# Late modulation groups on column quarters of TensorE, an earlier zero fill, and a merged exponent product in a diffusion-block kernel

## The chip, the core and the metric

The kernel runs on one core of a Trainium2 chip. A core has five engines, each with its own instruction queue that is worked off in order: TensorE (PE, matrix products; its weight loads are listed as PEld), VectorE (DVE), ScalarE (ACT), GpSimd (POOL) and SyncE (SP, which here issues nearly all DMAs; 16 DMA engines carry them out). Between engines only semaphores order the work. The metric is the time of one execution on the device in microseconds (us); the median of three runs of the kernel before is 1539.05 us.

## The reference, cut to what matters

One trunk layer over 256 context tokens and 1024 latent tokens of width 1024: adaptive modulation of a norm, one input projection (3096 columns) that feeds three head groups (RWKV-7, Mamba-2 SSD, gated linear attention, GLA), an output projection, and a mixture of experts.

```python
cond_l = jax.nn.silu(c); cond_c = jax.nn.silu(c_ctx)[None]
mod_l = jnp.split(cond_l @ ada_w[l] + ada_b[l], 6, -1)     # 1024 x 6144 weights
mod_c = jnp.split(cond_c @ ada_w[l] + ada_b[l], 6, -1)
hl = modulate(rmsnorm(x, norm1_g[l]), mod_l[0], mod_l[1])
hc = modulate(rmsnorm(ctx, norm1_g[l]), mod_c[0], mod_c[1])
mc, ml = mixer(hc, hl, ...)          # h @ w_in, then rwkv7 | ssd | gla, both directions
x = x + mod_l[2][:, None] * ml
x = x + mod_l[5][:, None] * hier_moe(modulate(rmsnorm(x, norm2_g[l]), mod_l[3], mod_l[4]), ...)
return rmsnorm(x, final_g)
```

The modulations are 6144 columns, worked in 12 groups of 512. Groups 0 to 3 (shift and scale of the first norm) are needed before anything else. Groups 4 to 11 (`mod_l[2]` to `mod_l[5]`) are needed only from the output projection on. In the SSD part, `decay_in = exp(a_cs[l] - a_cs[s])` over chunks of 128 tokens is the exponent product of the change.

## The kernel before

**Stages, by the profiled execution.** To 52 us inputs are loaded and transposed, the first four modulation groups computed (`ada_first`, L150, with plain matmuls at L163) and the first norm applied. From 52 to 564 us the projection stage runs (below). From 564 to 738 us the RWKV chain runs: 20 calls of `rw_step`, each a sequence of 64x64 matmuls on data that `rw_loads` (L575 on) fetches from DRAM (`cd`, `sm`, `v`), with GLA states and SSD states beside it. From 738 to 905 us `rw_finish`, `ssd_weights` and `gla_out` follow; then the output projection to about 1037 us, routing, and the experts from 1068 us to the end.

**The projection stage** is a list of jobs, the string PLAN. Job s is a block of RWKV heads (projections, then five calls of `rw_seg`, whose elementwise part is on DVE), z, q and c are projections (c with a 3x3 convolution on DVE, L739), g the gate, i the inversion of small triangular blocks (`rw_inverse`, 32x32 matmuls `px`), t the token-major projection (`pst`), and a is one late modulation group. Every fp32 projection is three matmuls on split operands (`mm3`, L261 to L263, result `psi` or `pst`); its weights come through `load_split`: a DMA into `wraw`, a tile of the pool wst with three buffers, then a split into `whi` and `wlo`. A framework schedules the instructions when the kernel is built: it simulates a timeline and writes each engine's order. On the chip each engine follows that order and waits where its next instruction is not ready.

**A late modulation group before** (`ada`, L178): four DMAs of 512 KB bring `wada`, which takes the same three buffers as `wraw`. DVE multiplies and adds the eight row blocks into `aacc` (one L188, seven L190), PE sums over partitions with four matmuls against a column of ones (`psa`, L193; each is two instructions), and L194 adds the bias. The eight groups stand between s0 and c0 in PLAN.

**Zeros and constants.** `rw_zeros` (L353) fills part of the DRAM tensor `sD` with zeros out of a tile of the pool tmp, which can only be opened once the pool st is closed. `ssd_consts2` (L947) then builds the constant part of `difD` (8 planes of 128x128 for each of 8 chunks) in `dift` and writes it. Both precede the first job.

**The exponent.** `ssd_dt` (L981) computes cumulated decays, splits each into three bf16 parts, and writes them into `difD` with 48 DMAs (L1056 to L1058). `ssd_weights` (L1115) loads `df` and makes the exponent of each direction as a mask product (L1135) plus two products over 36 rows (L1137, L1139), followed by the exponential on ACT (L1141).

## Time and profile before

| | us |
|---|---|
| median of 3 runs | 1539.05 (1538.52 to 1543.27) |
| the profiled execution | 1533.99 |
| its span (first to last instruction) | 1532.2 |
| PE busy in the span | 1340.5 (87%) |
| DVE busy | 785.2 (51%) |
| ACT busy | 515.4 (34%) |
| POOL busy | 389.5 (25%) |

The shares are averages over stages that have different limits, so they say little about one change. Of PE two things must be read beside its busy time: the clock that was granted in a stretch (1.00 is 2.4 GHz, 0.50 is 1.2 GHz), since at the lower level the same work shows twice the busy time; and whether the engine's next instruction was waiting, and for whom. Durations of single matmuls overlap with the next, so the step from one start to the next is the cost in a row of them.

### The profile page before, as it was taken

The numbers are of one execution on the slowest core, as the hardware profiler recorded it, in microseconds if no ns is written. First come the engines' busy times: TensorE is split into PE (matmuls) and PEld (weight loads), VectorE is DVE, ScalarE is ACT, GpSimd is POOL, SyncE is SP. The second block draws the span as 40 slices with busy tenths as digits, with TensorE's granted clock in tenths as the row PEclk, the third lists the DMA queues.
The fourth block names the chain that finished last, engine by engine and source line by source line (L and its number), as shares of the span: only waits on it lengthen the run. The fifth ranks groups of instructions, "written<-read, shape, count | busy, mean of one in ns | idle before, by whom it ended". The sixth has DMA issues, their size and how long they took to land. (4 is left out here: it accounts for less than half of the span.)

```text
span 1532.2 us, 28018 instructions
## 1 busy us (share of the span) xinstructions
PE 1340.5 (87%) x11077; PEld 1111.9 (73%) x11077; DVE 785.2 (51%) x1482; ACT 515.4 (34%) x1056; POOL 389.5 (25%) x432
## 2 busy tenths in 40 slices
PE   7897899999797776777889989993999999999984
PEld 3585677777676774666557767762999999999984
DVE  4849868889979854414564472227102212112532
ACT  5544334443363134422433352220212212212333
POOL 3312432343334111413453252112101111111112
PEclk9997899999899777889856589995999999999998
DMA  9454867677661467476544365425988868868984
GB/s 320 134 156 138 201 153 169 167 189 180 162 144 31 93 141 203 127 229 207 185 145 118 97 208 171 145 97 193 368 299 288 271 201 301 294 224 299 311 266 123
DMA packets 297253, 296.81 MB, mean 194 GB/s; under 512 B 114281, under 2 KB 214890, under 8 KB 297119
## 3 DMA queue, kind: packets, MB, share of 16 engines
q1 hardware_dynamic: 288095, 269.81, 57.7%
q0 software_dynamic: 7872, 20.97, 5.7%
q10 hardware_dynamic: 1152, 4.19, 0.7%
q8 instruction: 89, 1.46, 0.4%
q14 instruction: 45, 0.37, 0.1%
HBM read 221.44 MB, written 73.72 MB: 193 GB/s over the span
## 5 line engine op out<-in xcount | busy, mean ns | idle before, releaser
L1576 PE MATMUL p<-hT,w 128*128 128x144 f32 (+10 forms) x2048 | 263.2, 288 | 0.0
L1576 PEld LDWEIGHTS p<-hT,w 128*128 128x128 f32 x2048 | 257.6, 192 | 0.6
L262 PE MATMUL psi<-hlo,whi 128*128 128x512 f32 (+1 forms) x440 | 172.0, 391 | 5.0 <-DVE hlo L234 3.8
L261 PE MATMUL psi<-hhi,whi 128*128 128x512 f32 (+1 forms) x440 | 170.3, 389 | 0.0
L263 PE MATMUL psi<-hhi,wlo 128*128 128x512 f32 (+1 forms) x440 | 169.9, 387 | 0.3 <-POOL wlo L254 0.3
L1583 PE MATMUL p<-hid,w 128*128 128x144 f32 (+10 forms) x1024 | 136.6, 294 | 8.4 <-DVE hid L1578 7.2
L1583 PEld LDWEIGHTS p<-hid,w 128*128 128x128 f32 x1024 | 133.9, 199 | 9.0 <-DVE hid L1578 7.5
L1602 POOL DMA_INDIRECT acc<-yr,rows x27 | 41.4, 1532 | 323.0 <-DVE yr L1598 188.2
L1578 DVE TENSOR_TENSOR hid<-hid,p 128x144 f32<-128x144 f32 (+10 forms) x64 | 18.7, 294 | 170.0 <-PE p L1576 165.9
L262 PEld LDWEIGHTS psi<-hlo,whi 128*128 128x128 f32 x440 | 85.6, 195 | 26.0 <-DVE hlo L234 5.6
L263 PEld LDWEIGHTS psi<-hhi,wlo 128*128 128x128 f32 x440 | 85.4, 194 | 19.1 <-issue 3.4
L261 PEld LDWEIGHTS psi<-hhi,whi 128*128 128x128 f32 x440 | 85.8, 195 | 17.7 <-issue 2.1
L1598 DVE TENSOR_SCALAR yr<-pty,rows 128x512 f32<-128x512 f32 (+8 forms) x46 | 32.7, 741 | 112.4 <-PE pty L1592 105.2
L1584 ACT ACTIVATE yT<-p,mods 128x144 f32<-128x144 f32 (+10 forms) x128 | 43.0, 374 | 112.7 <-PE p L1583 112.5
L1577 ACT ACTIVATE hid<-p 128x144 f32<-128x144 f32 (+10 forms) x64 | 18.2, 284 | 168.8 <-PE p L1576 168.7
L739 DVE SCALAR_TENSOR_TENSOR co<-gr,pc,co 128x512 f32<-128x512 f32 x72 | 59.4, 849 | 6.5 <-ACT co L728 4.7
L190 DVE SCALAR_TENSOR_TENSOR aacc<-wada,csig,aacc 128x512 f32<-128x512 f32 x56 | 51.6, 921 | 15.6 <-DMA wada<-in_ada_w_dram 15.3
L262 PE MATMUL pso<-wol,mh 128*128 128x512 f32 x128 | 52.8, 412 | 3.3 <-DVE wol L1222 2.2
L261 PE MATMUL pso<-woh,mh 128*128 128x512 f32 x128 | 52.4, 412 | 1.0 <-DVE go L1265 1.0
L263 PE MATMUL pso<-woh,ml 128*128 128x512 f32 x128 | 52.6, 411 | 0.0
L463 PE MATMUL psg<-AR,BK 64*128 64x128 f32 x320 | 46.6, 304 | 4.0 <-DVE BK L456 1.6
L463 PEld LDWEIGHTS psg<-AR,BK 64*128 64x128 f32 x320 | 39.5, 204 | 13.4 <-issue 4.0
(540 smaller groups left out, 2668.3 us busy)
## 6 DMA issues: line engine op xcount, KB each, us to landing
w<-in_moe_w_dram SPq DMA_DIRECT2D x47, 2048.0 KB
wada<-in_ada_w_dram SPq DMA_DIRECT2D x32, 512.0 KB
cd<-stepD SPq DMA_DIRECT2D x20, 768.0 KB
wraw<-in_w_in_dram SPq DMA_DIRECT2D x24, 512.0 KB
aw<-in_ada_w_dram SPq DMA_DIRECT2D x10, 512.0 KB
stepD<-AR SPq DMA_DIRECT2D x40, 128.0 KB
mabD<-G SPq DMA_DIRECT2D x40, 128.0 KB
stepD<-G SPq DMA_DIRECT2D x40, 128.0 KB
```

Source lines behind the costliest of these rows:

```text
L190: nc.vector.scalar_tensor_tensor(acc, w[:, k % 2], g.sg[:, k, 0:1], acc, op0=OP.mult, op1=OP.add)
L261: nc.tensor.matmul(ps, whi(k), xhi(k), start=k == 0, stop=False)
L262: nc.tensor.matmul(ps, whi(k), xlo(k), start=False, stop=False)
L263: nc.tensor.matmul(ps, wlo(k), xhi(k), start=False, stop=k == 7)
L463: nc.tensor.matmul(pg[h][:, c, :], bkf[HS[h], c], arf[HS[h], c], start=True, stop=True)
L739: nc.vector.scalar_tensor_tensor(o, src(dy, dx), w(3 * dy + dx), o, op0=OP.mult, op1=OP.add)
L1576: nc.tensor.matmul(p[:, 0:n], w[:, k, fs], hT[:, k, s0:s0 + n], start=k == 0, stop=k == 7)
L1578: nc.vector.tensor_mul(hid[:, f, 0:n], hid[:, f, 0:n], p3[:, 0:n])
L1583: nc.tensor.matmul(p[:, 0:n], w2[:, f, 128 * k:128 * k + 128], hid[:, f, 0:n], start=f == 0, stop=f == 3)
L1584: nc.scalar.activation(yT[:, k, 0:n], p[:, 0:n], AF.Copy, scale=g.mods[:, 40 + k, 0:1])
L1598: nc.vector.tensor_scalar(yr[0:m, h], pf, wt[0:m, b:b + 1], None, op0=OP.mult)
L1602: nc.gpsimd.indirect_dma_start(out=g.acc, out_offset=bass.IndirectOffsetOnAxis(ap=rows[0:m, 0, b:b + 1], axis=0), in_=yr[0:m, :], in_offse ...
```

## The change

- **Late modulations on quarters.** `ada` no longer uses DVE. `sgz` holds the eight blocks of the condition vector, each widened to 32 columns of which only the first is not zero. A matmul with such a block as weights (128x32) and `wada` as the moving operand (128x512) uses a quarter of the array's columns, and block k goes to quarter k%4, partitions 32*(k%4) on, of one PSUM tile; so eight matmuls, two on each quarter, replace the eight DVE operations. ACT copies the tile to `arow`, four matmuls with `sel` (ones at partitions 0, 32, 64, 96) sum the quarters and turn the row into a column (`psc`), DVE adds the bias.
- **Where they stand.** In PLAN the groups 4 to 11 go from between s0 and c0 to between c0 and t0. `wada` moves from the pool wst to buffers of tmp that `rw_seg` no longer needs then (tags G, two, and kk, one).
- **Zeros.** The zero tile `z32` is a persistent one that DVE clears in `gla_consts`, so the `sD` fills don't wait for tmp; SP now issues them among the loads of `x` and `ada_w`. `ssd_consts2` comes after job s0.
- **Exponent.** Rows 36 to 47 of each 64-row half of `difD` carry what had planes 6 and 7. L1137 and L1139 become one product over 48 rows, and `difD` has 6 planes. `ssd_dt` writes its parts once to a DRAM tensor `partsD` and from there with 24 DMAs, DRAM to DRAM, into `difD`.

```diff
+    g.sgz = P.tile([128, 8, 32], F, name="sgz")
+    nc.gpsimd.memset(g.sgz, 0.0)
+    nc.vector.tensor_copy(g.sgz[:, :, 0:1], sg[:, :, 0:1])
+    g.sel = P.tile([128, 1], F, name="sel")
+    nc.vector.tensor_reduce(g.sel, g.ident[:, ::32], axis=AX.X, op=OP.add)
...
-def ada(g, grs):
-    for gr in grs:
-        acc = g.wst.tile([128, 512], F, tag="aacc", name="aacc", bufs=1)
-        for k in range(8):
-            if k % 2 == 0:
-                w = g.wst.tile([128, 2, 512], F, tag="wraw", name="wada", bufs=3)
-                nc.sync.dma_start(w, dap(g.a["ada_w"], 128 * 6144 * k + 512 * gr, [[6144, 128], [128 * 6144, 2], [1, 512]]))
-            if k == 0:
-                nc.vector.tensor_scalar(acc, w[:, 0], g.sg[:, 0, 0:1], None, op0=OP.mult)
...
-                nc.vector.scalar_tensor_tensor(acc, w[:, k % 2], g.sg[:, k, 0:1], acc, op0=OP.mult, op1=OP.add)
-        ps = g.ps.tile([128, 512], F, tag="mm", name="psa")
-        for j in range(4):
-            nc.tensor.matmul(ps[:, j:j + 1], acc[:, 128 * j:128 * j + 128], g.onesm[:, 0:1], start=True, stop=True)
+def ada(g, gr):
+    nc, W = g.nc, g.tmp
+    ps = g.ps.tile([128, 512], F, tag="tp", name="psa")
+    for k in range(8):
+        if k % 2 == 0:
+            g.nada = getattr(g, "nada", 0) + 1
+            if g.nada % 3:
+                w = W.tile([128, 1024], F, tag="G", name="wada", bufs=2)
             else:
+                w = W.tile([128, TT], F, tag="kk", name="wada", bufs=1)[:, 0:1024]
+            w = w.rearrange("p (k f) -> p k f", k=2)
+            nc.sync.dma_start(w, dap(g.a["ada_w"], 128 * 6144 * k + 512 * gr, [[6144, 128], [128 * 6144, 2], [1, 512]]))
+        o = slice(32 * (k % 4), 32 * (k % 4) + 32)
+        nc.tensor.matmul(ps[o, :], g.sgz[:, k, :], w[:, k % 2, :], start=k < 4, stop=k >= 4)
+    row = W.tile([128, 512], F, tag="sa", name="arow", bufs=2)
+    nc.scalar.activation(row, ps, AF.Copy)
+    pt = g.ps.tile([128, 4], F, tag="tp", name="psc")
+    for j in range(4):
+        nc.tensor.matmul(pt[:, j:j + 1], row[:, 128 * j:128 * j + 128], g.sel, start=True, stop=True)
+    nc.vector.tensor_add(g.mods[:, 4 * gr:4 * gr + 4, 0], pt, g.c("adab", 4 * gr, 4))
...
 def rw_zeros(g):
-    z = g.tmp.tile([32, 32], F, name="z32")
-    nc.gpsimd.memset(z, 0.0)
+    z = g.z32
...
-    g.difD = g.dram.tile([8, 128, 8, 128], BF, name="difD")
-    t = g.tmp.tile([128, 8, 128], BF, tag="rv", name="dift", bufs=1)
+    g.difD = g.dram.tile([8, 128, 6, 128], BF, name="difD")
+    t = g.tmp.tile([128, 6, 128], BF, tag="t1", name="dift", bufs=1)
...
+    pD = g.dram.tile([3, 128, 3, 128], BF, name="partsD")
+    nc.sync.dma_start(pD.rearrange("k p i t -> p k (i t)"), parts.rearrange("p k i t -> p k (i t)"))
     for d in range(2):
         for q in range(2):
             for h in range(4):
-                src = parts[64 * d + 4 * q + h:64 * d + 64:8]
-                o = 64 * q + 3 * h
-                nc.sync.dma_start(g.difD[:, o + 12 * d:o + 12 * d + 3, h], src[:, 0])
-                nc.sync.dma_start(g.difD[:, o + 24:o + 27, 4 + d], src[:, 2])
-                nc.sync.dma_start(g.difD[:, o + 24:o + 27, 6 + d], src[:, 1])
+                o = 64 * q + 12 * d + 3 * h
+                nc.sync.dma_start(g.difD[:, o:o + 3, h], pD[0, 64 * d + 4 * q + h:64 * d + 64:8])
+            for r, k in ((24, 2), (36, 1)):
+                nc.sync.dma_start(g.difD[:, 64 * q + r:64 * q + r + 12, 4 + d],
+                                  pD[k, 64 * d:64 * d + 64].rearrange("(c q h) i t -> q c (h i) t", q=2, h=4)[q])
...
-    K = [slice(64 * q, 64 * q + 36) for q in range(2)]
+    K = [slice(64 * q, 64 * q + 48) for q in range(2)]
...
         for q in range(2):
-            nc.tensor.matmul(pe[q].rearrange("p h t -> p (h t)"), df[K[q], 4 + d], R[q], start=False, stop=False)
-        for q in range(2):
-            nc.tensor.matmul(pe[q].rearrange("p h t -> p (h t)"), df[K[q], 6 + d], R[q], start=False, stop=True)
+            nc.tensor.matmul(pe[q].rearrange("p h t -> p (h t)"), df[K[q], 4 + d], R[q], start=False, stop=True)
...
-PLAN = "s0 a9 z0 a4 a5 z1 a7 s1 z3 q0 z2 a6 z5 z4 a11 q1 c1 a8 i0 g0 i2 a10 c0 c3 c2 c5 t0 i1 c4"
+PLAN = "s0 z0 z1 s1 z3 q0 z2 z5 z4 q1 c1 i0 g0 i2 c0 a4 a5 c3 a6 a7 c2 a8 a9 c5 a10 a11 t0 i1 c4"
...
-    ssd_consts2(g)
...
+    for i, job in enumerate(PLAN.split()):
+        if i == 1:
+            ssd_consts2(g)
```

What this does to the engines' orders is shown at three places. The line numbers of the changed kernel are 12 to 17 higher than those of the kernel before: L201 is the matmul on a quarter, L206 the sum with `sel`, L274 to L276 are `mm3`, L475 and L490 are L463 and L478 of before.

PE in the first RWKV block (`psl`, `ptv`, `psg`, `ptb` are steps of `rw_seg`), before:

```order
L426 MATMUL psl<-wa,wa_495 128x256
L193 MATMUL psa<-onesm,aacc 128x1 x4
L463 MATMUL psg<-AR,BK 128x128 x8
L426 MATMUL psl<-wa,wa_495 128x256 x2
L478 MATMUL ptb<-ident,BK 128x128 x4
L419 MATMUL ptv<-ident,rv 128x128 x2
L463 MATMUL psg<-AR,BK 128x128 x4
L426 MATMUL psl<-wa,wa_495 128x256
L463 MATMUL psg<-AR,BK 128x128 x4
L419 MATMUL ptv<-ident,sq 128x128 x2
L193 MATMUL psa<-onesm,aacc 128x1 x4
L261 MATMUL psi<-hhi,whi 128x512
```

The same place after:

```order
L275 MATMUL psi<-hlo,whi 128x512
L490 MATMUL ptb<-ident,BK 128x128 x4
L475 MATMUL psg<-AR,BK 128x128 x4
L438 MATMUL psl<-wa,wa_500 128x256
L431 MATMUL ptv<-ident,rv 128x128 x2
L276 MATMUL psi<-hhi,wlo 128x512
L274 MATMUL psi<-hhi,whi 128x512
```

Before, the steps of `rw_seg` stood bare, with two `psa` groups that need DVE's `aacc` between them; after, `psi` products of z0 and z1 stand between the steps (14 to 21 rows at a time), and no `psa`.

PE where the convolution projections end and the token-major projection begins, before:

```order
L261 MATMUL psi<-hhi,whi 128x512
L262 MATMUL psi<-hlo,whi 128x512
L263 MATMUL psi<-hhi,wlo 128x512
L261 MATMUL pst<-thi,hhi 128x280
L262 MATMUL pst<-tlo,hhi 128x280
```

and after:

```order
L274 MATMUL psi<-hhi,whi 128x512
L275 MATMUL psi<-hlo,whi 128x512
L206 MATMUL psc<-sel,arow 128x1 x4
L201 MATMUL psa<-wada,sgz 32x512 x6
L276 MATMUL psi<-hhi,wlo 128x512
L274 MATMUL pst<-thi,hhi 128x280
```

Eight such groups now stand in the last part of the stage. Four of them have their eight matmuls in pieces of 6 and 2, four in pieces of 4, 2 and 2, with `psi`, `pst` or `px` between.

SP in the RWKV chain, where the parts of the exponent are written, before:

```order
L582 DMA sm<-sD 128x2x128
L585 DMA sm<-mabD 128x2x64 x2
L588 DMA v<-vtD 64x4x64 x2
L580 DMA cd<-stepD 128x1536
L1056 DMA difD<-csp 8x3x128
L1057 DMA difD<-csp 8x3x128
L1058 DMA difD<-csp 8x3x128
```

and after:

```order
L592 DMA cd<-stepD 128x1536
L1092 DMA xt<-xsD 128x5x128
L1068 DMA partsD<-csp 128x3x384
L1073 DMA difD<-partsD 8x3x128 x4
L1075 DMA difD<-partsD 8x12x128 x2
L1073 DMA difD<-partsD 8x3x128 x3
L600 DMA v<-vtD 64x4x64 x2
L1073 DMA difD<-partsD 8x3x128
L1075 DMA difD<-partsD 8x12x128 x2
L1073 DMA difD<-partsD 8x3x128 x3
L592 DMA cd<-stepD 128x1536
```

Before, the 48 writes are spread over the loads of six chain steps; after, one write and 24 copies stand within the loads of two. In `ssd_weights` every L1139 is gone from PE's order. From the output projection on the orders of all engines are the same.

## Rows read from the trace of the kernel before

**Rows 1.** Windows: stretch, length, busy by engine (instructions), PE clock, DMA share, GB/s.

```profile
52.00:113.00 61.00, 55.64 (x266) 44.37 (x266) 41.63 (x47) 28.05 (x37) 16.91 (x25) 1.00 0.43 124
113.00:157.00 44.00, 32.81 (x143) 24.68 (x141) 41.09 (x58) 21.24 (x46) 11.77 (x16) 0.73 0.49 135
157.00:408.00 251.00, 238.00 (x1185) 182.92 (x1184) 214.50 (x354) 98.61 (x205) 88.68 (x97) 0.95 0.70 171
408.00:564.00 156.00, 124.90 (x1051) 109.67 (x1051) 127.28 (x237) 57.28 (x96) 41.45 (x50) 0.86 0.51 113
738.00:905.00 167.00, 153.11 (x1377) 101.74 (x1371) 93.59 (x167) 71.62 (x118) 67.86 (x63) 0.68 0.49 148
```

**Rows 2.** Groups of the page, and windows of line 190 alone (DVE).

```profile
L190 DVE SCALAR_TENSOR_TENSOR aacc<-wada,csig,aacc 128x512 f32<-128x512 f32 x56 | 51.6, 921 | 15.6 <-DMA wada<-in_ada_w_dram 15.3
...
52.00:408.00 356.00, 50.11 (x54) 0.93 0.63 159
```

**Rows 3.** Timeline of PE around the two `psa` groups: start, length, instruction, [idle before].

```profile
137.42 1.86 PE L193 MATMUL psa<-onesm,aacc 128*128 128x1 f32 x8 [3.08 <-DVE aacc L190]
...
156.01 1.87 PE L193 MATMUL psa<-onesm,aacc 128*128 128x1 f32 x8 [3.97 <-DVE aacc L190]
```

**Rows 4.** Timeline of SP's DMA issues before and after the zero fills.

```profile
65.03 0.37 SPq L186 DMA_DIRECT2D wada<-in_ada_w_dram  x1
75.80 3.10 SPq L359 DMA_DIRECT2D sD<-z  x4
...
92.23 1.30 SPq L250 DMA_DIRECT2D wraw<-in_w_in_dram  x1
```

**Rows 5.** Projections in a row on PE's timeline, and a window at the lower clock.

```profile
109.75 0.39 PE L261 MATMUL psi<-hhi,whi 128*128 128x512 f32 x1
...
113.02 0.40 PE L263 MATMUL psi<-hhi,wlo 128*128 128x512 f32 x1
...
133.00:164.00 31.00, 21.45 (x80) 16.84 (x81) 30.18 (x53) 10.55 (x28) 12.54 (x14) 0.50 0.75 200
```

**Rows 6.** Waits from 408 to 564 us: total, times, longest.

```profile
PE px L563 <- DMA t<-mabD: 16.1, 5, 6.6
PE pst L261 <- ACT gr L719: 8.3, 1, 8.3
...
SPq L743 <- DVE co L693: 32.3, 5, 12.1
```

**Rows 7.** PE's timeline: full-array fp32, two column halves, four quarters, change of tile size.

```profile
40.65 5.31 PE L163 MATMUL psa<-awr,csig 128*2 128x512 f32 x12
...
613.08 1.74 PE L1094 MATMUL pss<-xs,B 128*64 128x256 f32 x6
...
640.52 0.33 PE L859 MATMUL pkv<-vg,ke 64*32 64x64 f32 x12
...
447.16 1.11 PE L563 MATMUL px<-t,t 32*32 32x32 f32 x59
448.20 0.50 PE L262 MATMUL psi<-hlo,whi 128*128 128x512 f32 x1
```

**Rows 8.** RWKV chain: first and last write of the parts (SP), two waits of PE.

```profile
605.76 0.66 SPq L1056 DMA_DIRECT2D difD<-csp  x1
...
658.38 0.57 SPq L1058 DMA_DIRECT2D difD<-csp  x1
...
645.53 1.12 PE L596 MATMUL pa<-v,cd 64*64 64x64 f32 x16 [4.07 <-issue]
...
656.90 1.12 PE L596 MATMUL pa<-v,cd 64*64 64x64 f32 x16 [5.00 <-DMA cd<-stepD]
```

**Rows 9.** Exponent product: line 1139's ns (min/median/max), and PE's timeline at 880 us.

```profile
L1139 PE MATMUL pe<-df x32: 375/604/632, 757.5 to 895.2; 36*128 36x512 bf16 x32
...
880.33 0.39 PE L1137 MATMUL pe<-df 36*128 36x512 bf16 x1
880.55 0.38 PE L1139 MATMUL pe<-df 36*128 36x512 bf16 x1
```

More of the change, by code (lines that the diff above doesn't have):

```diff
@@ L786, in gla_consts @@
     nc.vector.tensor_copy(g.mA, f)
+    g.z32 = P.tile([32, 32], F, name="z32")
+    nc.vector.memset(g.z32, 0.0)
 def gla_states(g):
@@ L959, in ssd_consts2 @@
         for h in range(4):
-            nc.sync.dma_start(t[o + 24 + 3 * h:o + 27 + 3 * h, h], g.oneb[0:3])
+            for r in (24, 36):
+                nc.sync.dma_start(t[o + r + 3 * h:o + r + 3 + 3 * h, h], g.oneb[0:3])
     nc.sync.dma_start(g.difD.rearrange("c p i t -> p c (i t)"),
-                      t.rearrange("p i t -> p (i t)")[:, None].to_broadcast([128, 8, 1024]))
-    w = g.tmp.tile([128, 128], BF, tag="k2", name="dirt", bufs=1)
+                      t.rearrange("p i t -> p (i t)")[:, None].to_broadcast([128, 8, 768]))
+    w = g.tmp.tile([128, 128], BF, tag="t2", name="dirt", bufs=1)
     nc.gpsimd.memset(w, 0.0)
@@ L1121, in ssd_weights @@
     nc.sync.dma_start(xt, g.xsD[:, :, ts])
-    df = W.tile([128, 8, 128], BF, tag="df", name="df", bufs=2)
+    df = W.tile([128, 6, 128], BF, tag="df", name="df", bufs=2)
     nc.sync.dma_start(df, g.difD[tl - 2])
@@ L1798, in inverses @@
         rw_inverse(g, *(((0,), 4, 20), ((1,), 4, 20), ((0, 1), 0, 4))[j], nc.vector)
-    jobs = dict(z=z_proj, q=qk_proj, c=conv_proj, a=lambda g, j: ada(g, [j]), s=seg_block, i=inverses,
+    jobs = dict(z=z_proj, q=qk_proj, c=conv_proj, a=ada, s=seg_block, i=inverses,
                 g=lambda g, j: rw_gate(g, rw_proj(g, 7)), t=lambda g, j: tc_proj(g))
-    for job in PLAN.split():
+    for i, job in enumerate(PLAN.split()):
+        if i == 1:
+            ssd_consts2(g)
         jobs[job[0]](g, int(job[1:]))
```

2 lines of the change are left out of this document (removed).

## The prediction

> **What bounds the kernel now.** I read the stages first, in windows [rows 1], and in each the engine whose next work ends last. From the output projection on nothing is reordered, so the change must act before about 905 us. From 52 to 408 us (first projections, the RWKV segments, most of the late modulations) PE is busy 55.6 + 32.8 + 238.0 = 326 of 356 us and DVE 297 [rows 1]. To see how much of PE's time is work, I weight busy time by the granted clock: 55.6 x 1.00 + 32.8 x 0.73 + 238.0 x 0.95 = 306 us at 2.4 GHz; 50 of the 356 us are waiting or the lower clock. The worst stretch is 113 to 157 us, with 24 us of work in 44 us, and there DVE is busy 41 of 44 us: DVE sets the pace. Then the waits inside it: PE stands twice for `aacc`, 3.08 and 3.97 us [rows 3], and the clock falls to 0.50 from 133 to 164 us [rows 5], after PE had begun to idle. DVE spends 50.1 us of the stage on `aacc` [rows 2], and these operations stand in its order between those of `rw_seg`. Third, SP's queue: it issues a `wada` at 65.03 us, then nothing until the zero fills at 75.80 us, and the next `wraw`, which z1 needs, at 92.23 us [rows 4]; so PE had no other projections to put into the hole at 113 us.
>
> From 408 to 564 us PE is busy 125 of 156 us, at the upper clock 125 x 0.86 = 107, and DVE 127, with convolutions and the inversion. The named waits here are on a round trip through DRAM (`px`, 16.1 us) and on ACT (8.3 us) [rows 6]. No engine is full; it is a chain. In the RWKV chain the loads of `cd` come through SP's queue, and from 738 to 905 us PE is busy 153 of 167 us at a clock of 0.68 [rows 1], so work taken from it there counts.
>
> **Term 1, modulations off DVE (52 to 408 us): -22 us.** DVE falls from 297 to 297 - 50 = 247 us, well under PE. PE loses 56 of the 64 `psa` instructions; eight of them take 1.86 us at the lower clock [rows 3], so 0.12 each at the upper, 6.5 us. It gains 72 `psi` products that stood after 408 us; their step is (113.02 - 109.75) / 14 = 0.234 us [rows 5], 16.8 us. Work after: 306 - 6.5 + 16.8 = 316 us. If PE never waited, the stage would take 316 us (-40). If it kept the efficiency of the stretch from 157 to 408 us, where 238.0 x 0.95 = 226 us of work took 251 us (90%), it would take 351 us (-5). That stretch itself had DVE 85% busy (214.5 us), part of it with `aacc`. So I take 18 us of loss, about a third of today's 50: the waits for `aacc` and the hole at 113 to 157 us go, and z0 and z1 stand between the steps of the first block. 316 + 18 = 334, which is -22. Bounds: -5 and -40. The next late thing is PE itself.
>
> **Term 2, eight groups on quarters (408 to 564 us): -3 us.** One full-array fp32 instruction of 512 columns takes 5.31 / 12 = 0.44 us [rows 7]. 64 matmuls are 128 instructions, and one after another 128 x 0.44 = 56 us. Do quarters overlap? Twelve `pkv` instructions on quarters, 64 columns each, would take 12 x 0.055 = 0.66 us alone by this price; they take 0.33 us, most of it the last one's run [rows 7]: four run at once. Those have 64 rows. For 128 rows and two halves, six `pss` of 256 columns at the lower clock would take 6 x 0.44 = 2.6 us alone and take 1.74, about what pairs give [rows 7]. No row shows four streams of 128 rows, so the bounds are four at once and none at once. I take four, the nearest in shape of output: pieces of 6 and 2, or 4, 2 and 2, are six steps of 0.43 us a group, 2.6 us, and 20.5 us in all.
>
> Each piece also changes the tile size twice. By the row of a change (59 `px` of 0.016 us from 447.16 end at 448.10; the next `psi` starts at 448.20) this is 0.1 us, for 20 pieces and two changes 4 us, which I add. The Trainium skill (page TensorEngine Tiling (Array Packing), Key Properties) says that changing the tiling mode drains TensorE, which speaks against small pieces; without a drain this part of the sum would be 0 instead of 4 us.
>
> PE's work here is then 107 - 16.8 + 20.5 + 4 = 115 us, still far under 156. DVE loses the elementwise work of the moved projections: at the earlier stage's DVE time for PE's work, (297 - 50) / 306 = 0.8, that would be 14 us, but much of that belongs to the segments, and I take 10. PE's additions go into waits (24.4 us in the two named rows of rows 6) and keep its clock up. What could be lost is the loads: 32 of 512 KB, 16.8 MB, come into this stage. At the rate of the earlier stretch, 159 GB/s at a DMA share of 0.63 [rows 2], they are 16.8 MB / 252 GB/s = 67 us of all queues in 156 us, and the share rises from 0.51 to about 0.94 at worst. I take the 10 us of DVE and give back 7 for slower loads and ACT's copies. Bounds: -12 and +16.
>
> **Term 3, SP in the RWKV chain: -5 us.** 48 writes of 0.57 to 0.66 us between 605.76 and 658.38 us [rows 8] are 28 us of SP's 53. Now 25 DMAs, if they issue alike 15 us. PE's waits that go with it are 4.07 us (named issue, directly before a `pa` that needs `cd`) and 5.00 us for `cd` [rows 8], so 9 us can go. But the 25 now lie within two steps, the first copy waits until `partsD` has landed, and `v` and `cd` are queued behind it on SP; PE waits for them. I take half of the gain. Bounds: -10, and +4, the price of one more wait as in those rows. The Trainium skill (page DMA: Bandwidth & Descriptors, Anatomy of one DMA) gives about 2.0 us of fixed time for a DMA, told of GpSimd's path; no row here shows the copy, and by that figure alone the added landing would cost an estimated 2 us and the term would be -7.
>
> **Term 4, one exponent product: -6 us.** 32 instructions go. From L1137 to L1139 the step is 0.22 us at the upper clock [rows 9], twice that at the lower; the median length of L1139, 604 ns against 375 [rows 9], says that over half run at the lower. If each counts alone: 16 x 0.22 + 16 x 0.44 = 11 us; if the two halves of the rows always ran together, half of that. PE is busy 92% there [rows 1], so nearly all of it is on the path. 48 rows instead of 36 cost nothing in columns. I take 6, with bounds -2 and -10.
>
> **Term 5, zeros early: 0.** Four fills of 3.10 us of issue in all [rows 4] now stand among the loads before 52 us, whose queue is on the path; they might delay the first modulations, by 3 us at most if nothing hides them. In exchange SP isn't held from 65 to 76 us; that gain is part of term 1. The constants of `difD` come after job s0 and have until 605 us.
>
> **The sum.** -22 - 3 - 5 - 6 = -36. The profiled execution took 1534.0 us (span 1532.2), 5 us under the median of the three runs; so 1498 on its scale and 1539 - 36 = 1503 on that of the median. A difference under 0.3% (4.6 us) can't be told from none.
>
> **Rivals.**
> 1. *PE stays at 90% in the first stretch.* Then DVE was late there because PE was, and not the other way. For it: DVE has idle time even from 157 to 408 us (36 of 251 us); against it: the waits for `aacc` and the hole. Term 1 is -5, the sum -19: 1520 us.
> 2. *The hole closes wholly.* PE never waits and keeps 2.4 GHz: term 1 is -40, the sum -54: 1485 us. Against it: the first segment needs `rw_norm`, a chain on DVE, whatever stands beside it.
> 3. *Quarters run one after another.* 56 instead of 20.5 us: 36 more, of which the 31 us in which PE idles from 408 to 564 us hide perhaps 16. The sum is -16: 1523 us. For it: no row with 128 rows and four tiles.
> 4. *Late `wada`, slower than before.* PE's order is fixed, and a `psa` piece whose `wada` isn't there holds all projections and `px` behind it; SP's order is fixed too, and `wada` stands there behind stores of `xsD`, for which SP waited 32.3 us in 5 times, 6.5 us each, before [rows 6], and behind the freeing of only three buffers. If each of eight groups stands 6.5 us, that is 52 us: 1503 + 52 = 1555 us. It decides from 36 / 8 = 4.5 us a group on. Against it: the loads can run three ahead, and the order leaves mostly 12 to 30 products between pieces.
> 5. *The change doesn't do what it says.* The exponent with 48 rows or the DRAM hop might be no cheaper; terms 3 and 4 at their bad ends (+4, -2) leave -23: 1516 us, within the range.
>
> **How the numbers follow.** Forecast, 1492 to 1514 us: 0.48. Rival 1: 0.18. Rival 2: 0.14. Rival 3: 0.08. Rival 4: 0.08. Rival 5: 0.04. The range goes from 1482 us, in the middle of rival 2, to 1530 us, past rivals 1 and 3; it leaves out rival 4 and some of rival 2. Faster by over 0.3%: the forecast, rivals 1, 2, 5 and most of 3, 0.86; within 0.3%: 0.06 (rival 3 or 4 in part); slower: 0.08.
>
> **What would show it.** Term 1: in the changed profile the last segment product comes near 386 us instead of 408, DVE's share before it is under 80%, and the clock from 133 to 164 us is 1.00. Term 2: `psa` on quarters in steps of 0.43 us for four, and waits of PE for `wada` under 10 us in all; over 36 us is rival 4. Term 3: no wait of 4 to 5 us for `cd` after 640 us. Term 4: the exponential on ACT follows one product after the mask. It is wrong above all if the first stretch keeps its clock losses without DVE's work.

## The result and the profile after

The changed kernel took 1495.1 us (median of 4 runs, 1492.8 to 1499.0) against 1538.8 us of the kernel before in the same comparison: a ratio of 0.972 with a 95% interval of 0.968 to 0.976, or 43.7 us less. The forecast was 1503 us, 36 us less, and a range of 1482 to 1530 us. Its size was near and its direction right; the terms behind it were not all right, one of its reasons was only half of the truth, and some 15 us of the gain belong to no term.

The profiled execution of the changed kernel took 1493.6 us, its span is 1491.8 us, 40.4 us under the span before. I cut both spans at the same instructions on PE's timeline: the first `psi`, the last `ptb` of `rw_seg` (the end of the first stretch), the first and the last `pb` of the RWKV chain, the first `pso` of the output projection, the last `pn` before routing, and the last product of the experts.

| stretch (starts on PE) | before, us | after, us | difference | forecast |
|---|---|---|---|---|
| to the first projection | 51.6 | 55.6 | +4.0 | 0 (term 5) |
| first stretch, to the last `ptb` | 355.9 | 334.0 | -21.9 | -22 (term 1) |
| convolutions, to the chain's first `pb` | 161.1 | 166.3 | +5.2 | -3 (term 2) |
| RWKV chain, to its last `pb` | 167.3 | 156.0 | -11.3 | -5 (term 3) |
| SSD and GLA output, to the first `pso` | 169.7 | 157.4 | -12.3 | -6 (term 4) |
| output projection | 134.7 | 135.7 | +1.0 | 0 |
| routing and experts | 473.5 | 468.2 | -5.3 | 0 |

The windows of the changed kernel at these cuts (stretch, length, busy time of PE, PEld, DVE, ACT and POOL, PE clock, DMA share, GB/s), with the window of the hole of before, 133 to 164 us, as the last:

```profile
56.00:390.00 334.00, 320.88 (x1609) 248.04 (x1608) 253.85 (x396) 149.69 (x291) 110.34 (x132) 0.98 0.55 123
390.00:556.00 166.00, 146.91 (x1369) 110.33 (x1368) 119.43 (x233) 61.72 (x106) 37.37 (x53) 0.89 0.74 193
556.00:712.00 156.00, 117.97 (x2567) 97.75 (x2565) 67.15 (x150) 60.43 (x141) 45.61 (x47) 0.85 0.72 209
712.00:869.00 157.00, 142.13 (x1379) 100.12 (x1375) 97.24 (x165) 69.37 (x116) 68.42 (x62) 0.68 0.51 156
...
133.00:164.00 31.00, 31.00 (x166) 23.49 (x165) 24.39 (x42) 14.81 (x37) 12.49 (x15) 1.00 0.59 140
```

and those of the kernel before:

```profile
52.00:408.00 356.00, 326.44 (x1591) 251.97 (x1590) 297.22 (x457) 147.90 (x288) 117.36 (x137) 0.93 0.63 159
408.00:569.00 161.00, 129.90 (x1198) 114.42 (x1200) 127.97 (x238) 59.60 (x101) 41.95 (x50) 0.85 0.51 115
569.00:736.00 167.00, 125.40 (x2630) 102.86 (x2626) 62.67 (x145) 58.80 (x140) 42.31 (x43) 0.81 0.65 188
736.00:906.00 170.00, 156.11 (x1417) 103.92 (x1414) 94.87 (x169) 72.09 (x119) 68.69 (x64) 0.69 0.49 150
```

In the first stretch PE is now busy 321 of 334 us at a clock of 0.98, and the hole of before [rows 5] is full at 1.00. Busy time times clock is an estimate of PE's work: 326 x 0.93 = 304 us of 356 before and 321 x 0.98 = 314 of 334 after. What is left, the loss to waits and to the lower clock, fell from 52 to 20 us. In the convolutions PE is busy 147 instead of 130 us. In the SSD stage it is busy 14 us less. The removed products had 13.7 us of busy time (L1139), but that they account for the difference isn't shown: with them put back (experiment 9) PE is busy 147.5 us in this stage, only 5 us more than here.

PE's waits between 390 and 553 us (total, times, longest), and SP's:

```profile
PE px L575 <- DMA t<-mabD: 10.4, 2, 8.5
PE psa L201 <- DMA wada<-in_ada_w_dram: 4.2, 3, 2.1
...
SPq L199 <- PE psa L201: 14.6, 11, 4.4
```

PE stands 4.2 us for `wada`, not the 36 us of rival 4: SP and three buffers bring the loads in time. Against [rows 6] the round trip of `px` has shrunk from 16.1 to 10.4 us, and the wait for ACT's `gr` is gone. The pieces on quarters on PE's timeline (start, length), and the two new groups of the stretch (busy time, mean ns):

```profile
446.96 1.91 PE L201 MATMUL psa<-wada,sgz 128*32 128x512 f32 x12
...
453.01 0.29 PE L274 MATMUL pst<-thi,hhi 128*128 128x280 f32 x1
453.23 1.05 PE L201 MATMUL psa<-wada,sgz 128*32 128x512 f32 x4
454.21 0.40 PE L275 MATMUL pst<-tlo,hhi 128*128 128x280 f32 x1
...
506.90 1.07 PE L201 MATMUL psa<-wada,sgz 128*32 128x512 f32 x8
507.89 0.40 PE L275 MATMUL pst<-tlo,hhi 128*128 128x280 f32 x1
...
L201 PE MATMUL psa<-wada,sgz 128*32 128x512 f32 x128 | 27.3, 659 | 4.2 <-DMA wada<-in_ada_w_dram 4.2
...
L206 PE MATMUL psc<-sel,arow 128*128 128x1 f32 x64 | 8.6, 256 | 0.7 <-ACT arow L203 0.7
```

Six matmuls on quarters (12 instructions) take 1.91 us; at the 0.44 us of [rows 7] one after another they would take 5.3 us. Four quarters at 128 rows do run at once: a piece of four matmuls costs 507.89 - 506.90 = 0.99 us, and a piece of two 454.21 - 453.23 = 0.98 us, each two steps of 0.43 us and 0.12 us to change back, near the 0.1 us of [rows 7]. The Trainium skill (page TensorEngine Tiling (Array Packing), Key Properties) says that a change of the tiling mode drains TensorE. This trace agrees that a change costs time, and shows that it is little.

In the RWKV chain, SP's issues (start, length), and its wait at the first copy:

```profile
592.90 0.36 SPq L1068 DMA_DIRECT2D partsD<-csp  x1
595.18 2.74 SPq L1073 DMA_DIRECT2D difD<-partsD  x4
...
607.81 0.38 SPq L592 DMA_DIRECT2D cd<-stepD  x1
...
SPq L1073 <- DMA partsD<-csp: 1.8, 1, 1.8
```

The first copy is issued 2.28 us after the write: SP waits 1.8 us for `partsD` to land, as feared, but once. The Trainium skill (page DMA: Bandwidth & Descriptors, Anatomy of one DMA) gives about 2.0 us of fixed time, told of GpSimd's path. The wait in this trace, on SP's path, is near it.

### The profile page after: what moved, and what is told of

Its sections match the earlier page's. It is cut to its first block, busy times and chain, and to the rows that moved or that the text cites. A ratio compares the mean times of both kernels' runs of the same rounds, so it can differ in the third digit from the quotient of the medians.

```text
span 1491.8 us, 28106 instructions
## 1 busy us (share of the span) xinstructions
PE 1325.7 (89%) x11173; PEld 1089.7 (73%) x11173; DVE 742.0 (50%) x1421; ACT 517.6 (35%) x1062; POOL 381.3 (26%) x432
## 5 line engine op out<-in xcount | busy, mean ns | idle before, releaser
L275 PE MATMUL psi<-hlo,whi 128*128 128x512 f32 (+1 forms) x440 | 168.8, 384 | 3.2 <-DVE hlo L247 1.8
L274 PE MATMUL psi<-hhi,whi 128*128 128x512 f32 (+1 forms) x440 | 168.7, 385 | 0.7 <-ACT po L693 0.5
L276 PE MATMUL psi<-hhi,wlo 128*128 128x512 f32 (+1 forms) x440 | 167.5, 381 | 0.0
L1599 PE MATMUL p<-hid,w 128*128 128x144 f32 (+10 forms) x1024 | 133.0, 289 | 10.5 <-DVE hid L1594 8.1
L1599 PEld LDWEIGHTS p<-hid,w 128*128 128x128 f32 x1024 | 130.1, 193 | 11.2 <-DVE hid L1594 8.6
L274 PEld LDWEIGHTS psi<-hhi,whi 128*128 128x128 f32 x440 | 84.4, 192 | 21.3 <-issue 5.3
L276 PEld LDWEIGHTS psi<-hhi,wlo 128*128 128x128 f32 x440 | 84.4, 192 | 19.1 <-issue 4.5
L1593 ACT ACTIVATE hid<-p 128x144 f32<-128x144 f32 (+10 forms) x64 | 18.3, 285 | 166.9 <-PE p L1592 166.8
L751 DVE SCALAR_TENSOR_TENSOR co<-gr,pc,co 128x512 f32<-128x512 f32 x72 | 61.5, 872 | 13.2 <-ACT co L740 12.2
L274 PE MATMUL pso<-woh,mh 128*128 128x512 f32 x128 | 51.9, 408 | 2.6 <-DVE rb L1253 1.7
L276 PE MATMUL pso<-woh,ml 128*128 128x512 f32 x128 | 52.2, 408 | 0.0
L475 PE MATMUL psg<-AR,BK 64*128 64x128 f32 x320 | 45.8, 292 | 3.9 <-ACT BT L491 2.1
L1559 ACT ACTIVATE hT<-pte,mods,gs 128x128 f32<-128x128 f32 (+4 forms) x76 | 27.5, 448 | 61.9 <-PE pte L1555 61.9
L475 PEld LDWEIGHTS psg<-AR,BK 64*128 64x128 f32 x320 | 38.3, 194 | 14.1 <-issue 5.7
```

The lines of the kernel that those rows point to most:

```text
L274: nc.tensor.matmul(ps, whi(k), xhi(k), start=k == 0, stop=False)
L275: nc.tensor.matmul(ps, whi(k), xlo(k), start=False, stop=False)
L276: nc.tensor.matmul(ps, wlo(k), xhi(k), start=False, stop=k == 7)
L475: nc.tensor.matmul(pg[h][:, c, :], bkf[HS[h], c], arf[HS[h], c], start=True, stop=True)
L751: nc.vector.scalar_tensor_tensor(o, src(dy, dx), w(3 * dy + dx), o, op0=OP.mult, op1=OP.add)
L1559: nc.scalar.activation(hT[:, k, c0:c0 + m], pt[:, j, 0:m], AF.Identity, scale=g.gs2[:, k:k + 1], bias=g.mods[:, 24 + k, 0:1])
```

## The experiments

All times are medians with a comparison to the kernel before on the same chip. Where a kernel changes what is issued in the first 550 us, the framework's simulated timeline mostly changes too, and with it the orders of later stages, although their code is the same. So I read each experiment first in the stretch that it is meant for.

**1. Zeros and constants alone.** On the kernel before:

```diff
-    z = g.tmp.tile([32, 32], F, name="z32")
-    nc.gpsimd.memset(z, 0.0)
+    z = g.z32
...
-    ssd_consts2(g)
...
+        if i == 1:
+            ssd_consts2(g)
```

> The kernel before with one part of the change: the zero fills of sD come from a persistent tile among the first loads and the constants of difD come after job s0; the late modulations stay on VectorE at their old places. My theory (the stretch to the last RWKV segment got 22 us shorter because VectorE lost the 50 us of aacc work): that stretch shortens by 0 to 6 us, the start gets 4 us longer, total 1533 to 1541 us. Rival (it was SyncE, held from 65 to 76 us, so that z1's weights came late): the stretch shortens by 15 us or more, total 1520 to 1528 us.

Measured: 1549.1 us, ratio 1.006 (1.003 to 1.009). The first projection starts at 55.8 us (+4.2), the first stretch takes 357.9 us. Both totals that I had named were too low (the stages behind the first stretch got longer too), but the stretch tells the two apart: it is no shorter, and the rival falls. SP's queue shows why (start, length), with its largest wait at `wada` from 52 to 100 us (total, times, longest), and below it the queue of the changed kernel:

```profile
66.95 12.57 SPq L186 DMA_DIRECT2D wada<-in_ada_w_dram  x2
81.62 0.89 SPq L959 DMA_DIRECT2D dift<-oneb  x1
...
SPq L186 <- DVE aacc L190: 13.8, 2, 8.3
```

```profile
50.11 7.68 SPq L263 DMA_DIRECT2D wraw<-in_w_in_dram  x3
78.51 0.90 SPq L972 DMA_DIRECT2D dift<-oneb  x1
...
94.06 0.57 SPq L263 DMA_DIRECT2D wraw<-in_w_in_dram  x1
```

Without the zero fills SP stands as long at the next two `wada` loads, which find no free buffer. In the prediction I had read the gap from 65.03 to 75.80 us [rows 4] as the price of the fills; the loads of the late modulations would have held the queue anyway. Nor does the changed kernel free SP: it issues nothing from 57.79 to 78.51 us, the constants of `difD` still stand there, and the next `wraw` comes at 94.06 us, against 92.23 before. What differs is what it issued just before: `wraw` alone, and no `wada`.

**2. VectorE's method at the late places.** On the changed kernel, `ada` as before:

```diff
-        nc.tensor.matmul(ps[o, :], g.sgz[:, k, :], w[:, k % 2, :], start=k < 4, stop=k >= 4)
+                nc.vector.scalar_tensor_tensor(acc, w[:, k % 2], g.sg[:, k, 0:1], acc, op0=OP.mult, op1=OP.add)
```

> The changed kernel, but each late modulation group is computed by VectorE as before (wada in the three buffers of wraw, seven multiply-adds, four products with ones), at the new late places. My theory (VectorE bounds the first stretch, so moving its work away is enough there, but the last convolutions then pay for it): the first stretch is as short as in the changed kernel (334 us), the stretch after it grows from 163 to 170 to 185 us since VectorE has 117 + 50 us there; total 1502 to 1518 us. Rival (the place alone is what helps, the quarters only add TensorE work): the later stretch is no longer than 163 us, total 1495 us or less.

Measured: 1565.7 us, ratio 1.017 (1.013 to 1.022). First stretch 333.5 us, as in the changed kernel; the convolutions 213.2 us, far over what I expected. The window of that stretch and its longest wait:

```profile
390.00:603.00 213.00, 131.77 (x1245) 114.59 (x1246) 158.89 (x288) 61.15 (x102) 40.06 (x54) 0.73 0.59 148
...
PE psa L194 <- DVE aacc L191: 55.7, 3, 23.1
```

DVE is busy 159 of 213 us and PE stands 55.7 us for `aacc`. So moving the groups is enough for the first stretch, and the quarters are what makes the move affordable: at the late place they and the other buffers of `wada` (here the three of `wraw`) save 213 - 166 = 47 us.

**3. Quarters at the early places.** On the changed kernel, with the old PLAN and `wada` in the buffers of `wraw`:

```diff
-PLAN = "s0 z0 z1 s1 z3 q0 z2 z5 z4 q1 c1 i0 g0 i2 c0 a4 a5 c3 a6 a7 c2 a8 a9 c5 a10 a11 t0 i1 c4"
+PLAN = "s0 a9 z0 a4 a5 z1 a7 s1 z3 q0 z2 a6 z5 z4 a11 q1 c1 a8 i0 g0 i2 a10 c0 c3 c2 c5 t0 i1 c4"
...
+            w = g.wst.tile([128, 2, 512], F, tag="wraw", name="wada", bufs=3)
```

> The changed kernel with the quarters' matmuls, but at the old early places in the job list and with wada in the buffers of wraw. My theory (what counts is that VectorE is relieved): the first stretch pays some 27 us of TensorE work less what idles there, so it is 10 to 22 us longer than in the changed kernel, and the stretch after it 10 to 20 us shorter; total 1492 to 1505 us. Rival (the late place is what counts, since shared buffers and SyncE's order hold up z0 and z1): first stretch as long as before the change (356 us), total 1515 us or more.

Measured: 1671.8 us, ratio 1.084 (1.078 to 1.091). First stretch 377.0 us, and the convolutions 273.5, since much of the projections' work slipped behind. My expectation failed by far. This kernel shared PSUM buffers (tp) and ACT's copy buffers (sa) with the segments, which is a fault of its own, so I built it again without that.

**4. The same with other buffers** (results in the projections' PSUM buffers, ACT's copy in a tile of its own):

```diff
-    ps = g.ps.tile([128, 512], F, tag="tp", name="psa")
+    ps = g.ps.tile([128, 512], F, tag="mm", name="psa")
...
+        row = g.wst.tile([128, 256], F, tag="aacc", name="arow", bufs=1)
```

> The quarters at the old early places again, but without what the earlier kernel of that kind shared with the RWKV segments: the quarters' results go to the PSUM buffers of the projections (mm) instead of the segments' (tp), and ACT's copy goes, in two halves, to the tile that aacc had. Theory (relieving VectorE is enough; the earlier one was slow because its modulations and the segments waited for each other's buffers): first stretch 340 to 356 us against 334, the stretch after it 145 to 160 us against 166, total 1495 to 1520 us. Rival (loads of wada among the weights in SyncE's order and in the three buffers, with TensorE's fixed order, hold the projections wherever they stand early): first stretch 365 us or more, total 1560 us or more.

Measured: 1604.3 us, ratio 1.045 (1.039 to 1.050). First stretch 382.2 us: the rival holds. Its window, PE's longest wait in it, and three of SP's:

```profile
55.00:437.00 382.00, 341.54 (x1578) 248.06 (x1577) 237.98 (x386) 142.72 (x282) 100.33 (x125) 0.86 0.55 135
...
PE psi L271 <- ACT whi L262: 13.9, 2, 11.8
...
SPq L195 <- PE psa L197: 31.7, 6, 19.0
SPq L260 <- POOL wlo L264: 22.7, 3, 15.7
...
SPq L195 <- POOL wlo L264: 14.7, 1, 14.7
```

DVE is relieved (238 us busy of 382) and the stretch is 48 us longer than in the changed kernel. SP stands 31.7 + 14.7 us at `wada` (L195) for a buffer and 22.7 us at `wraw` (L260): weights and `wada` take turns in three buffers, and PE's granted clock is 0.86 on average.

**5. VectorE's time alone.** On the kernel before, the seven multiply-adds of each group on 8 of 512 columns; the modulations are then incomplete, the routing differs, and only the time up to the experts can be compared:

```diff
-                nc.vector.scalar_tensor_tensor(acc, w[:, k % 2], g.sg[:, k, 0:1], acc, op0=OP.mult, op1=OP.add)
+                nc.vector.scalar_tensor_tensor(acc[:, 0:8], w[:, k % 2, 0:8], g.sg[:, k, 0:1], acc[:, 0:8], op0=OP.mult, op1=OP.add)
```

> The kernel before, with VectorE's seven multiply-adds of each late modulation group cut to the first 8 of 512 columns, so that the modulations are incomplete; all loads of wada, their buffers, their places in the job list and the products with ones stay. It parts the two things that the change took out of the first stretch at once: VectorE's 50 us, and 16.8 MB of loads in the projections' buffers. Theory (VectorE's time): the first stretch falls from 356 us to 330 to 345 us, total 1512 to 1528 us. Rival (the loads and their buffers, as the slow kernels with quarters at the early places suggest): the first stretch stays at 350 us or more, total 1532 us or more.

Measured: 1818.4 us in all, of which the experts with their other routing take 769.6; the first stretch is 351.7 us, which is what the rival said. Its window:

```profile
52.00:404.00 352.00, 330.48 (x1650) 257.35 (x1649) 270.78 (x473) 149.97 (x292) 113.44 (x138) 0.95 0.67 167
```

4 us shorter, and with 46 more `psi` products in it (1030 instead of 984), 10.7 us of work. By busy time times clock the loss is 352 - 330 x 0.95 = 38 us, against 52 before and 20 in the changed kernel. So VectorE's time was about 14 of the 32 us that PE got back, a rough split, as this kernel has an order of its own; the other 18 go with the loads in the projections' buffers and with the places.

The hole of before shows it more directly. Of 113 to 157 us, these are the instructions with `psi` (busy time of PE, PEld and ACT, then PE's clock, DMA share, GB/s), and the `wraw` that SP issues from 60 to 145 us (ns, first and last start): before, in this kernel, and in that of experiment 2.

```profile
113.00:157.00 44.00, 13.09 (x50) 8.71 (x48) 1.77 (x3) 0.73 0.49 135
L250 SPq DMA_DIRECT2D wraw<-in_w_in_dram x1: 1296/1296/1296, 92.2 to 92.2; - x1
...
113.00:157.00 44.00, 16.94 (x61) 11.54 (x59) 2.75 (x5) 0.77 0.61 180
L250 SPq DMA_DIRECT2D wraw<-in_w_in_dram x2: 378/866/1353, 92.2 to 139.8; - x2
...
113.00:157.00 44.00, 36.27 (x154) 26.81 (x153) 3.32 (x6) 1.00 0.36 96
L251 SPq DMA_DIRECT2D wraw<-in_w_in_dram x5: 368/383/1463, 94.4 to 135.0; - x5
```

With VectorE's operations cut short, PE has 61 products there against 50 before; with the loads of `wada` moved away and VectorE's method kept, it has 154, as in the changed kernel, since five loads of weights come instead of one or two. So the hole closes with the weights. Whether `wada` kept them back in SP's order or in the three buffers isn't parted here, and DVE, still busy 38 of the 44 us in this kernel, is not ruled out as a part of it.

**6. One quarter for all eight blocks.**

```diff
-        o = slice(32 * (k % 4), 32 * (k % 4) + 32)
+        o = slice(0, 32)
```

> The changed kernel with all eight matmuls of a group on the first quarter of the array, so that none can overlap another; ACT copies 32 rows and the sum is over these. If quarters run four at once: the group's matmuls take 55 us in all instead of 27, TensorE has 19 us of waits in that stretch (163 us) to hide some of it, so the stretch is 12 to 25 us longer, total 1507 to 1520 us. Rival (TensorE isn't the bound there, or the quarters did not overlap): no difference, 1493 to 1498 us.

Measured: 1542.0 us, ratio 1.001 (0.998 to 1.004). A piece of 12 instructions and the group:

```profile
445.75 5.34 PE L201 MATMUL psa<-wada,sgz 128*32 128x512 f32 x12
...
L201 PE MATMUL psa<-wada,sgz 128*32 128x512 f32 x128 | 60.7, 610 | 3.2 <-DMA wada<-in_ada_w_dram 3.2
```

5.34 instead of 1.91 us, 60.7 instead of 27.3 us in all, and the stretch takes 187.5 instead of 166.3 us (+21.2, in the expected 12 to 25). That is less than half of the loss of 47 us, with which the total missed the expected 1507 to 1520 us. The rest arose behind it, where the code is the same: from the chain's first `pb` to the first `pso` 328.4 instead of 313.4 us, the output projection +7.5, the experts +6.7. Two windows of this kernel, chain and SSD stage (the like of the changed kernel stand in the section before):

```profile
577.00:737.00 160.00, 113.10 (x2487) 95.72 (x2487) 54.02 (x131) 52.52 (x124) 40.37 (x41) 0.87 0.67 199
737.00:905.00 168.00, 143.68 (x1456) 97.88 (x1452) 106.08 (x187) 78.85 (x135) 74.18 (x68) 0.70 0.46 141
```

The order of the changed kernel puts 67 us of DVE's work beside the chain, this one 54, and does 106 instead of 97 us behind it.

**7. The changed kernel again**, as a reference for the next three.

> The changed kernel once more, unchanged, so that the three runs beside it have it on the same chip and the stages show how much they vary by themselves. Theory: 1493 to 1499 us, stages as in its first profile within 2 us each, the experts perhaps 468 to 475 us. Rival (the gain behind the first projections was partly a lucky execution): RWKV chain and SSD stage nearer to those of before, 160 and 172 us.

Measured: 1491.9 us, ratio 0.969 (0.965 to 0.972). Stretches 334.1, 165.8, 154.9, 156.6, 135.8, 468.8 us: within 1.1 us of the first profile. Experiment 10 turned out to be a third execution of the same orders, and there the chain takes 153.0 and the experts 471.0 us. So with orders held, single stages still differ by up to 3 us, and a difference between two profiles has to be larger than that to say anything.

**8. 48 writes instead of one write and 24 copies.**

```diff
-    pD = g.dram.tile([3, 128, 3, 128], BF, name="partsD")
...
+                nc.sync.dma_start(g.difD[:, o + 12 * d:o + 12 * d + 3, h], src[:, 0])
+                nc.sync.dma_start(g.difD[:, o + 24:o + 27, 4 + d], src[:, 2])
+                nc.sync.dma_start(g.difD[:, o + 36:o + 39, 4 + d], src[:, 1])
```

> The changed kernel with the parts of the exponent written by 48 DMAs straight from VectorE's tile, as before the change, in place of one write to DRAM and 24 copies; the orders are the same up to the RWKV chain. Theory (SyncE's issue time set the pace of the chain's loads): the chain takes 6 to 14 us more than with the copies, total 1501 to 1510 us. Rival (the chain got shorter for another reason, such as the order that the schedule gave it): within 3 us, 1493 to 1499 us.

Measured: 1497.1 us, ratio 0.973 (0.969 to 0.976): 5.2 us more than the changed kernel beside it, in the chain 160.1 against 154.9. The chain's 5.2 us lie under the 6 to 14 that I expected and over the 3 of the rival, in whose range the total is. DVE, ACT and POOL have the changed kernel's orders here, row by row, so this is the cleanest of the comparisons. The copies are worth about 5 us in the chain, just what term 3 had; but the SSD stage behind it is 3.7 us shorter (152.9 against 156.6), so that both together take 313.0 us, against 309.2 to 313.4 in the three executions of the changed kernel's orders. Where the 5.2 us between the medians lie in the end isn't shown; 2.2 are in the output projection (138.0 against 135.8).

**9. Two products for the exponent.**

```diff
-    K = [slice(64 * q, 64 * q + 48) for q in range(2)]
+    K = [slice(64 * q, 64 * q + 36) for q in range(2)]
...
+            nc.tensor.matmul(pe[q].rearrange("p h t -> p (h t)"), df[K[q], 6 + d], R[q], start=False, stop=True)
```

> The changed kernel with two products over 36 rows for each direction's exponent, as before the change, and eight planes in difD; the orders are the same up to the stage after the RWKV chain but for a few rows. Theory (32 products on TensorE's path at 0.22 to 0.44 us): that stage takes 6 to 11 us more, total 1501 to 1507 us. Rival (the products were hidden, the stage's gain came from its order): within 3 us.

Measured: 1508.9 us, ratio 0.981 (0.977 to 0.985), 17.0 us more than the changed kernel; the two profiles differ by 13.2 us. The SSD stage, and the group in it:

```profile
712.00:872.00 160.00, 147.50 (x1418) 98.41 (x1414) 96.71 (x161) 71.55 (x119) 70.34 (x63) 0.71 0.48 147
...
L1157 PE MATMUL pe<-df 36*128 36x512 bf16 x32 | 13.5, 473 | 0.0
```

Only 3.3 us are in the stage that I named (159.9 against 156.6). The chain has 4.2 more, the output projection 4.2, the experts 3.3. But the orders of all engines are the changed kernel's until 15 us behind the chain: the first row of PE that differs starts at 727 us there, and the chain ends at 712. So a new order can't have made the chain longer, and no run says what did. The removal is worth more than forecast, and most of that lies outside the stage of the products.

**10. The fills behind s0 by place in the program.**

```diff
-    rw_zeros(g)
...
+            rw_zeros(g)
             ssd_consts2(g)
```

> The changed kernel with the zero fills of sD moved from the first loads to behind job s0, out of the same persistent tile; only SyncE's order and a few places on ScalarE differ. Theory (the fills stand among the loads of x and ada_w and make the first projection 4 us later): first projection at 51 to 53 us instead of 55.6, total 3 to 5 us less, 1489 to 1493 us. Rival (something else made the start later, or SyncE now holds back z0's weights): first projection unchanged, or the gain is lost in the first stretch, 1495 us or more.

Measured: 1491.2 us, first projection at 55.5 us. It told nothing of the fills: the framework moved them forward again, as SP's queue shows, and the order of every engine is that of the changed kernel, row by row. So it is one more execution of that kernel (stages 334.2, 165.4, 153.0, 156.1, 135.8, 471.0 us).

```profile
21.87 1.54 SPq L371 DMA_DIRECT2D sD<-z  x2
23.51 2.52 SPq L169 DMA_DIRECT2D aw<-in_ada_w_dram  x1
```

**11. The fills behind s0 by their buffer** (the zero tile in a buffer of tmp that the constants use first):

```diff
-    z = g.z32
+    z = g.tmp.tile([32, 32], F, tag="t1", name="z32", bufs=1)
+    nc.vector.memset(z, 0.0)
```

> The changed kernel with the zero tile in a buffer of tmp behind the constants of difD, so that the fills of sD can't be issued before job s0 has begun (with the persistent tile the schedule had put them among the first loads again). The orders of the first stretch differ in many rows. Theory (the fills delay the loads of ada_w and so the first projection by 4 us): first projection at 51 to 53 us instead of 55, total 3 to 5 us less than the changed kernel, 1487 to 1490 us on the chip of the last runs, if the rest is alike. Rival (the late start has another cause): first projection at 55 us.

Measured: first projection at 51.7 us, so the fills do cost the 4 us at the start. The total is 1505.7 us, ratio 0.981 (0.975 to 0.986), all the same: the orders changed, and the chain, the SSD stage, the output projection and the experts took 3.0, 5.3, 2.9 and 5.0 us more than in experiment 7, of which only the SSD stage and the experts are clear of the 3 us.

**12. The groups beside the RWKV chain.**

```diff
+    M.open("right", "ad")
...
+    for gr in range(4, 12):
+        ada(g, gr)
     rw_finish(g)
```

> The changed kernel with all eight late modulation groups behind the RWKV chain in the program, with own buffers, so that the schedule puts their matmuls among the chain's steps. Theory (TensorE is the bound at the end of the convolutions, where the quarters cost 27 us of it, and it waits in the chain): the stretch of the convolutions is 14 to 25 us shorter than 166 us, the chain 5 to 15 us longer than 155 us, total 5 to 15 us less than the changed kernel. Rival (the chain's loads have no room beside 16.8 MB of wada, the DMA queues are at 0.72 there): the chain grows by 20 us or more, total no less than the changed kernel.

Measured: 1559.2 us, ratio 1.015 (1.009 to 1.021). The convolutions fall to 150.1 us, as expected; the chain grows to 173.1, and the SSD stage to 213.5 us: the rival holds. A window of the chain (the DMA share is the last but one number), and two waits:

```profile
530.00:630.00 100.00, 84.27 (x1474) 56.15 (x1470) 6.06 (x18) 19.40 (x48) 7.61 (x13) 0.83 0.91 290
...
PE pa L603 <- DMA cd<-stepD: 17.9, 8, 8.5
PE psa L196 <- DMA wada<-in_ada_w_dram: 9.7, 6, 4.4
```

The queues are at 0.91, DVE has 6 us of work in 100 us, and its SSD and GLA work comes after the chain. Of use is the first number: with no late group at all, the first projection to the first `pb` takes 484.4 us. Before the change it was 517.0, after it 500.4. By this the eight groups cost 33 us there before, and 16 us now.

None of the twelve beats the changed kernel by more than its own spread.

## Why the prediction was right or wrong

**Term 1, -22, measured -21.9.** The size came from 316 us of work and 18 us of loss; it was 314 and 20. The work was worked out, but the 18 us were a choice between two bounds 35 us apart, and no row gave them: that they fit to 2 us is partly luck. The cause was put too simply: I wrote that DVE sets the pace. What counts is where the groups stand. All kernels with the late places have 333.5 to 336.3 us in this stretch, with quarters or with VectorE's method, and all with the early ones 351.7 to 382.2 us. VectorE's time is about 14 of the 32 us of loss that went (experiment 5). That the rest goes with the loads is shown by the hole (the `psi` of experiment 5) and, in direction, by experiments 1 and 4 (SP stands for buffers, and quarters at the early places make the stretch longer, not shorter); how it splits between buffers, SP's order and the schedule's choice is open, since most of those kernels also had an order of their own. The signs that I had named came (the last segment product at 389.7 us, DVE busy 76%, the clock at 1.00 in the hole), but they would have come with either cause.

**Term 2, -3, measured +5, within its bounds.** The pieces cost 27.3 us against 20.5 + 4, as forecast but for one row: I left out the sums with `sel`, which run 64 instructions as `psa` did before, and here take 8.6 us of PE. With them PE's work in the stretch is 147 x 0.89 = 131 us and not 115 (118 with the cuts of the table), and the waits that were to hide it had shrunk to 166 - 147 = 19 us. Of 33.4 us more for `psa` 21.2 show in the stretch (experiment 6), and of the 35.9 us of `psa` and `psc` 16.2 go when they go (experiment 12), about half of PE's time either way; so the sums alone make an estimated 4 to 5 of the 8 us by which the term missed. Rival 3 priced one quarter at 20 us more than the forecast (1523 against 1503); experiment 6 has 21 in the stretch itself.

**Term 3, -5, measured -5.2 in the chain by experiment 8**, of the 11.3 us by which the chain got shorter, and most of it given back in the stage behind. What the rest of the 11.3 us goes with is taken up below.

**Term 4, -6, measured 17 by experiment 9, beyond its bound of -10.** The step that failed is the one that put the term into one stage, and took PE's busy share of 92% there to mean that work taken from PE shortens that stage. The direct part in the stage is 3.3 us, at the low end, and some 12 us lie in the chain, the output projection and the experts, which I had not thought of as a cost at all; why is open (experiment 9).

**Chain and SSD stage together, -11 by terms 3 and 4, measured -23.6** (337.0 us before, 313.4 after). Leaving out the copies makes them 313.0 us, leaving out the single product 319.0. The kernels of experiments 2, 3, 4 and 6 have the copies and the single product too, in other orders: they take 327.4 to 329.7 us there, and their SSD stages 166.8 to 169.7, as long as before the change (169.7). That of experiment 5 has neither and takes 327.2 us, its SSD stage 156.4. So the shorter SSD stage isn't shown to come from the removed products, and some 15 us of the gain hang on the order that the schedule happened to give these two stages. No term of the prediction had that; it is luck.

**Term 5, 0, measured +4.** I named 3 us as the most that the fills could cost, and took 0 because a gain on SP stood against it. The gain did not exist (experiment 1; the changed kernel's SP is held as long), and the cost did (experiment 11).

**The rest.** The experts took 5.3 us less. I had written that from the output projection on the orders are the same; by the traces a few rows differ, in the output projection and at the start of the experts (on PE they are the same from 1081 us on before, and from 1044 us after). Over the kernels with intact modulations the experts took 467.9 to 477.1 us, and 468.2 to 471.0 in three executions of the same orders, so most of the 5.3 us is unexplained. The forecast came as near as it did by luck: terms 2 and 5, 12 us too good, stood against terms 3 and 4 and the experts, some 18 us too small by stages.

## What to carry to other kernels

Work that is not needed soon can free the stage that it leaves, when its loads share buffers and a queue with work that is needed: look for the queue's waits at those loads, not only at the engine that computes. Where it goes it has to fit: VectorE's method at the late places won the first stretch and lost 47 us behind it. Before a part is called done, count every instruction that it still leaves, as the small sums that follow a cheaper product. And where a schedule is made from a simulated timeline, an edit worth 4 us can cost other stages 16 (experiment 11): measure stage by stage, compare the orders row by row, and keep them fixed where one cause is to be told from another.

## What the runs showed of the hardware

Four matmuls of 128 rows and 32 columns each, on the four column quarters, ran in the time of two on two quarters (0.99 and 0.98 us to the next start); 12 instructions of 512 columns took 1.91 us on four quarters, against 5.34 us on one. Going from full-array products to quarters and back cost about 0.1 us each way. A DMA from DRAM to DRAM that had to follow a write to DRAM was issued 2.28 us after it, 1.8 us of which SP waited for the landing.
